# Bias matmuls over 128 rows, the softmax exchange spaced out, and an earlier turn of two x tiles, in a two-layer hybrid decoder

## The chip, the cores and the metric

The kernel runs on one core of a Trainium2 chip. The core has a matmul engine (TensorE, PE in the profile; its weight loads are listed as PEld), VectorE (DVE), ScalarE (ACT), GpSimd (POOL) and a sync engine (SP) that here only issues transfers. Each engine works through its own instructions in order; they meet at semaphores. Transfers are issued on the queues of SP, POOL and ACT. The metric is the time of one launch on the device, in microseconds (us), lower being better.

## The reference

Two layers over one sequence of 512 tokens of width 1024, in fp32. What matters here:

```
z = x @ w_in + b_in                    # 1024 -> 11648 columns, then split
q_a, k_a, v_a, q_r, k_r, v_r, g_r, gate_a, gate_b = split(z)
# (A) three groups of 6 heads of 64: causal windows (128, dilation 1), (512, 4), (2048, 16)
o_g, lse_g = attention(q_a, k_a, v_a)  # per group: output and log of the softmax denominator
y_a = sum_g softmax(lse)_g * o_g       # groups weighed by their denominators
# (B) retention, 4 heads: rotated q, k of 256, v of 512, chunks of 128, group norm
y_b = silu(g_r) * retention(q_r, k_r, v_r)
merged = sigmoid(gate_a) * (y_a @ w_attn_proj) + sigmoid(gate_b) * (y_b @ w_ret_proj)
x = layer_norm(alpha * x + merged @ w_out)
x = layer_norm(alpha * x + (silu(x @ w_gate) * (x @ w_up)) @ w_down)   # 2816 wide
```

The biases b_in are eight times as large as drawn, so they count in the result.

## The kernel before

**Numbers in two parts.** An fp32 value is held as a high part, rounded to the fast matmul format (fp32r), and a low part, the rest. `hilo` (L91) makes them: ScalarE casts the high part (L92), VectorE subtracts it from the source (L93). A product then takes three matmuls (`mm3`, L83): high by high, high by low, low by high. All of them go through the one line L81. x is held transposed as `xh` and `xl`, weights in `whi` and `wlo` (4 buffers each), loaded to `raw` (8 buffers of 512 KB). The source only gives an order of preference: a planner at compile time places each instruction on its engine's list by what its cost model thinks is ready.

**Seven products for eight.** The columns for v (attention) and for v and the swish gates (retention) are made by `tall` (L358): a Strassen form with seven products of half size. `ORDER` (L290) lists them: the left factors are parts of x or sums of such (`xs`), the right ones are the loaded blocks B11, B21, B22 and the sums P1 (B11 and B12), P2, P3 (B12 and B22) and P4. `Right` (L295) loads them on SP's queue; P1 and P3 are summed by a second, accumulating load on POOL's queue (L310), P2 and P4 by VectorE (L336) in P1's buffer. In `begin` (L332) all loads are asked for at once, B22 ahead of P3; B22 is the right factor of the fourth product and P3 that of the sixth. Three accumulators run along (`CHAIN`, L292), each opened by its first product.

**The bias.** It is added by one more matmul at the head of two of the chains (L369 to L371): `ones` as the stationary operand and `bh` as the moving one. Only two of their 33 rows hold anything: row 0 has the high part of the bias, row 32 the low part, and `ones` is 1 in these two rows and 0 elsewhere. `bias_rows` (L399) makes `bh`: POOL clears 33 rows (L403), four small transfers bring the two bias rows (L405, L406), VectorE adds (L407), ScalarE casts (L409), VectorE makes the low part in row 32 alone (L411). Each call of `biased` has 4 such matmuls; it is called twice a layer for attention's v (288 columns, the V stage) and four times for retention (512 columns): 48 in all.

**Side work.** Attention's own steps are threaded between weight matmuls: they stand in a list `side`, and `tick` (L133) takes from it at a rate that `pace` sets as steps per us. Attention runs in 3 pairs of heads (hp). For each pair `attention_pair` makes steps `scores` (L476: matmuls, VectorE's minimum L492, ScalarE's Exp L494), `turn` (L497: transposes, ScalarE copies to `sT` L503) and `values` (L506: matmuls, copies to `y` L513), and then weighs the two orders of tokens in which its groups run against each other. Tokens of the two orders sit on different partitions, so the statistics go through DRAM and back (the exchange), on ScalarE's queue:

- `swap` (L522) writes maxima and sums (L527); `swapped` reads them in the other order (L530) to `mb`.
- `weigh` (L532): VectorE's L536 to L538, ScalarE's Exp L539, VectorE's L540 to L544, a write of the weights `wb` (L545), and VectorE's `fa` for the first order (L546).
- `weighed` (L548) reads the weights in the other order (L549).
- `scale(0)`, `scale(1)` (L553) multiply `y` by them; `place(0)`, `place(1)` (L555) transpose `y` (L558) and put or add it into `yaT` (L560, L563).

The steps from `swapped` on are the tail; a pair's tail is worked in among the steps of the next pair at fixed places (L776), and the last pair's tail during the first retention head (L782).

**The start of layer 0** (L677 to L710). SP loads two x tiles, the four 128-column parts of the first q/k weights, the third x tile, the weights of the second group, and the fourth x tile. `to_xT` (L159) turns an x tile in two halves: four transposes, the cast of `xh`, the subtraction for `xl`, and a copy `xc` (L174) that is needed later for the sums. The first weights' parts are cast in `pair_units` (L196) when their loads are asked for; then tile 0 is turned, and tile 1 is the first entry of the side list, taken when the first matmul needs it (`need`, L151).

Of the kernel before, what the change touches and what calls it, by code (L numbers as in the profile page):

```python
# [18 lines left out]
P = 128  # L19
# [26 lines left out]
NEG = -1e30  # L46
L0, L1 = 383, 255
WARM = 3
BK = 33
FPARTS = ((0, 6), (6, 14), (14, 22))  # L50


# [1 line left out]
def hybrid_kernel(ctx, tc, x, rel_bias, w_in, b_in, w_attn_proj, w_ret_proj, w_out,  # L54
# [12 lines left out]

    ident = keep.tile([P, P], F32, name="ident")
    mhalf = keep.tile([P, 1], F32, name="mhalf")
    ones = keep.tile([BK, P], F32R, name="ones")  # L70
    bh = keep.tile([BK, 1024], F32R, name="bh")
    xh = keep.tile([P, KD, S], F32R, name="xh")
    xl = keep.tile([P, KD, S], F32R, name="xl")
    xs = keep.tile([P, 4, 2, 4, 256], F32R, name="xs")
# [16 lines left out]
    def hilo(src, hi, lo):  # L91
        act.copy(out=hi, in_=src)  # L92
# [11 lines left out]
    def view(t, a, b):  # L104
        return t[:, :a * b].rearrange("p (a b) -> p a b", a=a)
# [6 lines left out]
    def unit(v):  # L112
        a, b = v.shape[1], v.shape[2]
        h = view(wp.tile([P, 1024], F32R, tag="whi", name="whi"), a, b)
        l = view(wp.tile([P, 1024], F32R, tag="wlo", name="wlo"), a, b)
        hilo(v, h, l)
        return h, l
# [75 lines left out]
        return [[view(raw("xc"), 4, 256) for _ in range(2)] for _ in range(2)]  # L193


    def pair_units(w, c, c2=None, apart=False):  # L196
# [9 lines left out]
        if c2 is not None:  # L206
            todo = [(hf, q) for hf in range(2) for q in range(2)]
            for hf, q in sorted(todo, key=lambda t: t[::-1]) if apart else todo:
                nc.sync.dma_start(vs[hf][:, :, q * P:(q + 1) * P], w[:, 4 * hf:4 * hf + 4, (c, c2)[q]:(c, c2)[q] + P])
        if not apart:  # L210
            return [unit(v) for v in vs]
        out_ = [tuple(view(wp.tile([P, 1024], F32R, tag=t, name=t), 4, 256) for t in ("whi", "wlo")) for _ in vs]
        for q in range(2):
            for v, (h, l) in zip(vs, out_):
                cs = slice(q * P, (q + 1) * P)
                hilo(v[:, :, cs], h[:, :, cs], l[:, :, cs])
        return out_

    def part_of(us, k, q):
        h, l = us[k // 4]  # L220
# [74 lines left out]
    class Right:  # L295
# [33 lines left out]
        def begin(self, n):  # L329

            if n == "B11":
                self.load("B11", "B21", "P1", "B22", "P3")  # L332
            elif n in ("P2", "P4"):
                for u in range(len(self.shapes)):
                    r = self.t["P1", u]
                    dve.tensor_tensor(out=r, in0=r, in1=self.t["B22" if n == "P2" else "B21", u], op=ALU.add)  # L336
            return self.high(n)
# [61 lines left out]
    def bias_rows(b1, b2):  # L399

        n = b1.shape[0]
        r = raw("rb")[:BK, :2 * n]
        pool.memset(r, 0.0)  # L403
        for q in (0, BK - 1):
            pool.dma_start(r[q:q + 1, :n], b1.unsqueeze(0))  # L405
            pool.dma_start(r[q:q + 1, n:], b2.unsqueeze(0))  # L406
        dve.tensor_tensor(out=r[:, n:], in0=r[:, n:], in1=r[:, :n], op=ALU.add)  # L407
        h = bh[:, :2 * n]
        act.copy(out=h, in_=r)  # L409
        e = slice(BK - 1, BK)  # L410
        dve.tensor_tensor(out=h[e], in0=r[e], in1=h[e].bitcast(F32), op=ALU.subtract)  # L411
        return h

# [55 lines left out]
    def attention_pair(hp, qk, v, yp, bias, yaT):  # L469
# [104 lines left out]
            if t == 0:  # L574
                ops += [nothing] * 2
        ops.append(swap)
        tail = [swapped, weigh, weighed, lambda: scale(0), lambda: place(0), lambda: scale(1), lambda: place(1)]
        return ops, tail

    VB = 288  # L580
# [12 lines left out]
    def layer(ly, cp):  # L593
# [65 lines left out]
        with stage("attn") as ap_, stage("attw", 4) as aw:  # L659
# [2 lines left out]
            def qk_slot(hp, g):  # L662
                qk[hp, g] = opp.tile([P, 2, S], F32, tag="op", name="qk")

            def qk_units(hp, g, apart=False):
                c = g * GW + hp * P
                return pair_units(w_l, C_QA + c, C_KA + c, apart)

            def qk_put(hp, g, j, ps):
                cc = (C_QA, C_KA)[j] + g * GW + hp * P  # L670
# [6 lines left out]
            if ly == 0:  # L677
                x0 = [slot("x0", F32) for _ in range(NI)]
                warm = work("warm")
                dve.memset(warm, 0.0)  # L680
                px = psum()

                for _ in range(WARM):
                    mm(px, warm[:, :P], warm, True, True)
                act.dma_start(ident, c_id)

                def load_x(i):
                    for hf in range(2):
                        nc.sync.dma_start(x0[i][:, hf], x[i * P:(i + 1) * P, hf * S:(hf + 1) * S])

                load_x(0)
                load_x(1)
                for l_ in range(DEPTH):
                    pool.dma_start(braws[l_], b_in[l_].rearrange("(a b) -> a b", b=P))
                vecs = bias_vectors([aw.tile([P, S], F32, tag="bias", name="hot") for _ in range(NG)])
                us0 = [qk_units(0, 0, True)]
                load_x(2)
                us0.append(qk_units(0, 1))
                load_x(3)
                cp = x_copies()  # L700
                ops = [to_xT(x0[i].rearrange("p a b -> p (a b)"), i, cp) for i in range(NI)]
                for f in ops[0]:
                    f()
                side.extend(ops[1] + [lambda l_=l_: bias_cols(l_) for l_ in range(DEPTH)] + vecs[:3] + ops[2] + vecs[3:] + ops[3])
                o32 = work("o32")
                dve.memset(o32[:BK, :P], 0.0)
                dve.memset(o32[0:1, :P], 1.0)
                dve.memset(o32[BK - 1:BK, :P], 1.0)
                act.copy(out=ones, in_=o32[:BK, :P])
                rate[0], credit[0] = 0.4, 0.0  # L710
            else:
                us0 = [qk_units(0, g) for g in range(2)]
# [386 lines left out]
```

## Time and profile before

| what | value |
|---|---|
| time, median of 3 runs | 2248.61 us (2247.89 to 2251.42) |
| the profiled execution | 2250.18 us |
| its span, first to last instruction | 2248.4 us |
| TensorE busy | 2223.7 us (99%), 10890 matmuls |
| VectorE, ScalarE, POOL busy | 1184.3, 844.7, 180.8 us |
| mean granted TensorE clock | 0.997 |
| HBM traffic | 131 GB/s over the span |

Times in a timeline are us from the span's start: a row gives the start, the busy time, the engine, the line and operation, what is written from what, the tile's shape, and in brackets how long the engine was idle before it and what ended that. TensorE's matmuls overlap in their pipeline, so a row's busy time is longer than the distance to the next start; the distance is what the engine spends on it. A letter q after an engine marks its queue of transfers. In a table of stretches the columns are the stretch, its length, the busy time and count of PE, PEld, DVE, ACT and POOL, the granted clock as a share of full speed, the busy share of the DMA engines and the GB/s moved.

### The profile page before, as it was taken

What the parts mean: (1) busy time and instruction counts of PE and PEld (TensorE: products, weight loads), DVE (VectorE), ACT (ScalarE), POOL (GpSimd) and SP (SyncE); (2) the same over time, 40 slices, a digit from 0 to 9 for tenths busy, and PEclk for the clock granted to TensorE, in tenths of its full rate; (3) what the DMA queues carried; (4) which work ended last, traced back from release to release, by engine and by line L of the source; (5) the groups of instructions that cost most, each with busy time, mean ns of one, the idle gap of its engine ahead of it and who ended that gap; (6) DMA issues with size and microseconds to landing.
All of it is one profiled execution on the core that took longest, in us unless ns stands there. A gap on an engine that the chain in (4) does not pass through costs nothing.

```text
span 2248.4 us, 27714 instructions
## 1 busy us (share of the span) xinstructions
PE 2223.7 (99%) x10890; PEld 1841.0 (82%) x10890; DVE 1184.3 (53%) x1795; ACT 844.7 (38%) x1373; POOL 180.8 (8%) x240
## 2 busy tenths in 40 slices
PE   8999999999999999999999999999999999999998
PEld 7977778878888888888889777788888888888886
DVE  5643677776245543334376446777743455333345
ACT  4444544545333132223145445445543232222230
POOL 3110011110000100000030100111000001000001
PEclk9999999999999999999999999999999999999999
DMA  7943365555655133333159343565455552333320
GB/s 213 240 128 83 74 161 151 140 133 158 216 178 187 57 113 94 94 95 111 47 155 248 98 91 86 146 167 144 125 172 195 193 169 66 101 89 101 103 76 38
DMA packets 261602, 294.23 MB, mean 131 GB/s; under 512 B 21517, under 2 KB 199841, under 8 KB 261344
## 3 DMA queue, kind: packets, MB, share of 16 engines
q1 hardware_dynamic: 212928, 234.13, 35.0%
q0 software_dynamic: 21264, 45.54, 9.1%
q10 hardware_dynamic: 27280, 12.80, 2.0%
q8 instruction: 85, 1.39, 0.3%
q14 instruction: 45, 0.37, 0.1%
HBM read 266.63 MB, written 28.53 MB: 131 GB/s over the span
## 4 chain that ended last, share of the span: by engine, by line
PE 74%; issue 16%; DMA 4%; DVE 3%; POOL 1%; ACT 1%; POOLq 0%; DVEq 0%; ACTq 0%
PE ps L81 66%; PE px L81 6%; DMA raw<-in_w_in 2%; PE px L502 1%; POOL ry L124 1%; PE px L833 1%; DMA exd<-wb 1%; DMA fa<-exd 1%; DVE wlo L325 1%; DVE xtok L926 1%; DMA rb<-in_b_in 0%; DMA exd<-pk 0%; DMA mb<-exd 0%; DVE stats L937 0%; PE px L169 0%
## 5 line engine op out<-in xcount | busy, mean ns | idle before, releaser
L81 PE MATMUL ps<-xh,whi 128*128 128x512 f32 (+1 forms) x1760 | 674.8, 385 | 7.1 <-ACT xh L92 7.1
L81 PE MATMUL ps<-xh,wlo 128*128 128x512 f32 (+1 forms) x1760 | 659.7, 375 | 1.0 <-DVE wlo L93 1.0
L81 PE MATMUL ps<-xl,whi 128*128 128x512 f32 (+1 forms) x1760 | 659.6, 375 | 0.2 <-DVE xl L93 0.2
L93 DVE TENSOR_TENSOR wlo<-raw,whi 128x1024 fp32r<-128x1024 f32 (+2 forms) x274 | 330.8, 1208 | 528.2 <-ACT whi L92 527.7
L92 ACT CAST whi<-raw 128x1024 fp32r<-128x1024 f32 (+2 forms) x274 | 282.8, 1035 | 462.9 <-PE ps L81 399.6
L81 PEld LDWEIGHTS ps<-xh,whi 128*128 128x128 f32 x1760 | 332.1, 189 | 71.3 <-ACT xh L92 8.3
L81 PEld LDWEIGHTS ps<-xh,wlo 128*128 128x128 f32 x1760 | 332.2, 189 | 61.2 <-DVE wlo L93 1.2
L81 PEld LDWEIGHTS ps<-xl,whi 128*128 128x128 f32 x1760 | 333.1, 189 | 53.7 <-DVE xl L93 1.0
L81 PE MATMUL ps<-whi,xs 128*128 128x512 f32 (+1 forms) x768 | 221.9, 363 | 0.0
L325 DVE TENSOR_TENSOR wlo<-raw,whi 128x1024 fp32r<-128x1024 f32 (+1 forms) x168 | 178.7, 1064 | 81.1 <-ACT whi L319 80.3
L319 ACT CAST whi<-raw 128x1024 fp32r<-128x1024 f32 (+1 forms) x168 | 154.2, 923 | 118.8 <-PE ps L81 92.6
L81 PE MATMUL ps<-whi,ht 128*128 128x512 f32 x576 | 178.3, 389 | 0.0
L81 PEld LDWEIGHTS ps<-whi,xs 128*128 128x128 f32 x768 | 137.7, 188 | 24.1 <-ACT whi L319 2.2
L81 PE MATMUL ps<-wlo,xs 128*128 128x512 f32 (+1 forms) x384 | 138.0, 359 | 0.4 <-DVE wlo L325 0.4
L124 POOL TENSOR_TENSOR ry<-ve,mhalf 128x1 f32<-128x1 f32 x48 | 44.8, 944 | 1152.0 <-DVE ve L123 1152.0
L81 PEld LDWEIGHTS ps<-whi,ht 128*128 128x128 f32 x576 | 108.1, 188 | 22.4
L81 PE MATMUL ps<-wlo,ht 128*128 128x512 f32 x288 | 112.0, 389 | 0.0
L81 PE MATMUL ps<-whi,xh 128*128 128x512 f32 (+1 forms) x288 | 106.7, 370 | 1.9 <-DVE sn L429 1.9
L81 PE MATMUL ps<-wlo,xh 128*128 128x512 f32 (+1 forms) x288 | 103.2, 358 | 0.0
L81 PE MATMUL ps<-whi,xl 128*128 128x512 f32 (+1 forms) x288 | 103.0, 358 | 0.0
L310 POOL DMA_DIRECT2D raw<-in_w_in x48 | 59.2, 1234 | 293.0 <-DMA raw<-in_w_in 204.0
L81 PEld LDWEIGHTS ps<-wlo,xs 128*128 128x128 f32 x384 | 72.2, 188 | 9.6 <-DVE wlo L325 0.9
(167 smaller groups left out, 2518.9 us busy)
## 6 DMA issues: line engine op xcount, KB each, us to landing
raw<-in_w_in SPq DMA_DIRECT2D x144, 512.0 KB, 4.0
raw<-in_w_ffn_gate SPq DMA_DIRECT2D x44, 512.0 KB, 3.8
raw<-in_w_ffn_up SPq DMA_DIRECT2D x44, 512.0 KB, 3.8
raw<-in_w_ffn_down SPq DMA_DIRECT2D x44, 512.0 KB, 3.7
raw<-in_w_in SPq DMA_DIRECT2D x72, 256.0 KB, 5.3
raw<-in_w_in POOLq DMA_DIRECT2D x32, 512.0 KB, 7.4
raw<-in_w_ret_proj SPq DMA_DIRECT2D x32, 512.0 KB, 3.9
raw<-in_w_in SPq DMA_DIRECT2D x40, 288.0 KB, 4.3
```

The costliest lines, as they stand in the source:

```text
L81: pe.matmul(ps, lhsT=a, rhs=b, start=start, stop=stop, skip_group_check=True)
L92: act.copy(out=hi, in_=src)
L93: dve.tensor_tensor(out=lo, in0=src, in1=hi.bitcast(F32), op=ALU.subtract)
L124: pool.tensor_tensor(out=y, in0=ve, in1=mhalf, op=ALU.pow)
L310: pool.dma_start(r, self.src({"P1": "B12", "P3": "B22"}[n], u), accum_op=ALU.add)
L319: act.copy(out=h, in_=src)
L325: dve.tensor_tensor(out=l, in0=src, in1=h.bitcast(F32), op=ALU.subtract)
L502: pe.transpose(px[:, (2 + j) * P:(3 + j) * P], s[:, hh, j * P:(j + 1) * P], ident)
L833: pe.transpose(px[:, t * P:(t + 1) * P], ys[i][:, t * P:(t + 1) * P], ident)
L926: dve.scalar_tensor_tensor(out=o_, in0=o_, scalar=rs, in1=b_[:, c:c + n], op0=ALU.mult, op1=ALU.add)
```

## The change

Four things are edited.

- The tiles `ones` and `bh`, the cleared raw tile and its casts have 128 rows. Row 0 and row 32 hold the same as before, the other rows are zero.
- The tail's steps have another order and other places: `scale(0)` and `place(0)` now come before `weighed`. Among the next pair's steps `weigh` is put in at 12, not 8, `weighed` at 18, not 12, and the rest at 14, 16, 24 and 26; after the last pair there are more empty steps between.
- At the start of layer 0 tiles 0 and 1 of x are both turned before the first weights' parts are cast; the loads are asked for in the same order as before. The parts' function is now `pair_apart`, which gives the casts back as a function to be called later.
- In `begin`, P3 is loaded ahead of B22.

```diff
-BK = 33
+BK = 32
...
-    ones = keep.tile([BK, P], F32R, name="ones")
-    bh = keep.tile([BK, 1024], F32R, name="bh")
+    ones = keep.tile([P, P], F32R, name="ones")
+    bh = keep.tile([P, 1024], F32R, name="bh")
...
+    def pair_apart(w, c, c2):
+
+        vs = [view(raw(), 4, 256) for _ in range(2)]
         out_ = [tuple(view(wp.tile([P, 1024], F32R, tag=t, name=t), 4, 256) for t in ("whi", "wlo")) for _ in vs]
-        for q in range(2):
-            for v, (h, l) in zip(vs, out_):
-                cs = slice(q * P, (q + 1) * P)
-                hilo(v[:, :, cs], h[:, :, cs], l[:, :, cs])
-        return out_
+        parts = [(hf, slice(q * P, (q + 1) * P), cc) for q, cc in enumerate((c, c2)) for hf in range(2)]
+        for hf, cs, cc in parts:
+            nc.sync.dma_start(vs[hf][:, :, cs], w[:, 4 * hf:4 * hf + 4, cc:cc + P])
+
+        def make():
+            for hf, cs, _ in parts:
+                hilo(vs[hf][:, :, cs], out_[hf][0][:, :, cs], out_[hf][1][:, :, cs])
+
+        return out_, make
...
-                self.load("B11", "B21", "P1", "B22", "P3")
+                self.load("B11", "B21", "P1", "P3", "B22")
...
-        r = raw("rb")[:BK, :2 * n]
+        r = raw("rb")[:, :2 * n]
         pool.memset(r, 0.0)
-        for q in (0, BK - 1):
+        for q in (0, BK):
...
-        e = slice(BK - 1, BK)
+        e = slice(BK, BK + 1)
...
-        tail = [swapped, weigh, weighed, lambda: scale(0), lambda: place(0), lambda: scale(1), lambda: place(1)]
+        tail = [swapped, weigh, lambda: scale(0), lambda: place(0), weighed, lambda: scale(1), lambda: place(1)]
...
-                us0 = [qk_units(0, 0, True)]
+                first, make = qk_units(0, 0, pair_apart)
                 load_x(2)
-                us0.append(qk_units(0, 1))
-                load_x(3)
                 cp = x_copies()
                 ops = [to_xT(x0[i].rearrange("p a b -> p (a b)"), i, cp) for i in range(NI)]
-                for f in ops[0]:
+                for f in ops[0] + ops[1]:
                     f()
-                side.extend(ops[1] + [lambda l_=l_: bias_cols(l_) for l_ in range(DEPTH)] + vecs[:3] + ops[2] + vecs[3:] + ops[3])
+                make()
+                us0 = [first, qk_units(0, 1)]
+                load_x(3)
+                side.extend([lambda l_=l_: bias_cols(l_) for l_ in range(DEPTH)] + vecs[:3] + ops[2] + vecs[3:] + ops[3])
                 o32 = work("o32")
-                dve.memset(o32[:BK, :P], 0.0)
+                dve.memset(o32[:, :P], 0.0)
                 dve.memset(o32[0:1, :P], 1.0)
-                dve.memset(o32[BK - 1:BK, :P], 1.0)
-                act.copy(out=ones, in_=o32[:BK, :P])
+                dve.memset(o32[BK:BK + 1, :P], 1.0)
+                act.copy(out=ones, in_=o32[:, :P])
...
-                for at, f in zip((24, 22, 15, 14, 12, 8, 3), reversed(tail)):
+                for at, f in zip((26, 24, 18, 16, 14, 12, 3), reversed(tail)):
...
-            side.extend(n * 3 + tail[:1] + n * 4 + tail[1:2] + n * 3 + tail[2:5] + n * 6 + tail[5:6] + n * 2 + tail[6:])
+            side.extend(n * 3 + tail[:1] + n * 8 + tail[1:2] + n + tail[2:3] + n + tail[3:4] + n * 3 + tail[4:5] + n * 7 + tail[5:6] + n * 2 + tail[6:])
```

More of the change, by code (lines that the diff above doesn't have):

```diff
@@ L193, in x_copies, with pair_units @@
         return [[view(raw("xc"), 4, 256) for _ in range(2)] for _ in range(2)]
-    def pair_units(w, c, c2=None, apart=False):
+    def pair_units(w, c, c2=None):
         vs = []
@@ L205, in pair_units @@
                 vs.append(view(raw(), 4, 256))
[L206 to L211, printed above, removed]
-        out_ = [tuple(view(wp.tile([P, 1024], F32R, tag=t, name=t), 4, 256) for t in ("whi", "wlo")) for _ in vs]
-        for q in range(2):
-            for v, (h, l) in zip(vs, out_):
-                cs = slice(q * P, (q + 1) * P)
-                hilo(v[:, :, cs], h[:, :, cs], l[:, :, cs])
-        return out_
+                for q, cc in enumerate((c, c2)):
+                    nc.sync.dma_start(vs[hf][:, :, q * P:(q + 1) * P], w[:, ks, cc:cc + P])
+        return [unit(v) for v in vs]
+    def pair_apart(w, c, c2):
+        vs = [view(raw(), 4, 256) for _ in range(2)]
+        out_ = [tuple(view(wp.tile([P, 1024], F32R, tag=t, name=t), 4, 256) for t in ("whi", "wlo")) for _ in vs]
+        parts = [(hf, slice(q * P, (q + 1) * P), cc) for q, cc in enumerate((c, c2)) for hf in range(2)]
[5 more added lines that the diff above has]
+        return out_, make
     def part_of(us, k, q):
@@ L663, in qk_slot, with qk_units @@
                 qk[hp, g] = opp.tile([P, 2, S], F32, tag="op", name="qk")
-            def qk_units(hp, g, apart=False):
+            def qk_units(hp, g, how=pair_units):
                 c = g * GW + hp * P
-                return pair_units(w_l, C_QA + c, C_KA + c, apart)
+                return how(w_l, C_QA + c, C_KA + c)
             def qk_put(hp, g, j, ps):
```

## The prediction

> **What bounds the kernel now.** I read the cores, then the engines on the page, then the groups of the tile "bh", and then the timeline of each engine at the places that the diff touches.
>
> ```profile
> core 0: 2248.4 us, clock 0.997
> PE 2223.7 (99%) x10890; PEld 1841.0 (82%) x10890; DVE 1184.3 (53%) x1795; ACT 844.7 (38%) x1373; POOL 180.8 (8%) x240
> ```
>
> TensorE bounds it. Its 99% is made of modelled, overlapping ends, so lost time doesn't show there; it shows in the distance from one matmul's start to the next. An edit is worth what it takes out of these distances, and work on another engine counts only where TensorE waits for it. The profiled execution took 2250.18 us round its span of 2248.4; it is 1.57 over the median of the runs, 2248.61.
>
> **The bias matmuls: -18.9 us.** First a chain that opens without a bias (the second row), then the same with one:
>
> ```profile
> 334.79 0.39 PE L81 MATMUL ps<-whi,xl 128*128 128x512 f32 x1
> 335.02 0.39 PE L81 MATMUL ps<-whi,xh 128*128 128x512 f32 x1
> 335.25 0.39 PE L81 MATMUL ps<-wlo,xh 128*128 128x512 f32 x1
> ...
> 340.23 0.39 PE L81 MATMUL ps<-whi,xl 128*128 128x512 f32 x1
> 340.55 0.50 PE L81 MATMUL ps<-bh,ones 33*128 33x512 f32 x1
> 340.98 0.50 PE L81 MATMUL ps<-whi,xs 128*128 128x512 f32 x1
> 341.31 0.39 PE L81 MATMUL ps<-wlo,xs 128*128 128x512 f32 x1
> ```
>
> Two steps from 334.79 to 335.25 take 0.46, 0.23 each, and opening a new chain (335.02) costs nothing. Three steps from 340.23 to 341.31 take 1.08. So one bias matmul of 512 columns costs 0.40 us (1.08 less three of 0.227, the unrounded step) beyond its own place. With 288 columns, in the V stage:
>
> ```profile
> 87.53 0.29 PE L81 MATMUL ps<-wlo,xh 128*128 128x288 f32 x1
> 87.67 0.29 PE L81 MATMUL ps<-whi,xl 128*128 128x288 f32 x1
> 87.89 0.39 PE L81 MATMUL ps<-bh,ones 33*128 33x288 f32 x1
> ...
> 88.45 0.30 PE L81 MATMUL ps<-wlo,xs 128*128 128x288 f32 x1
> ```
>
> From 87.67 to 88.45 are 0.78 against three steps of 0.133 (as from 87.53 to 87.67): 0.38 lost. How many there are, and the work that prepares their rows:
>
> ```profile
> L81 PE MATMUL ps<-bh,ones x48: 393/498/502, 56.0 to 1603.1; 33*128 33x512 f32 x32, 33*128 33x288 f32 x16
> L409 ACT CAST bh<-rb x12: 669/1043/1050, 49.5 to 1546.4; 33x1024 fp32r<-33x1024 f32 x8, 33x576 fp32r<-33x576 f32 x4
> ```
>
> 32 x 0.40 + 16 x 0.38 = 18.9 us, all of it in TensorE's own order, with no other engine named ahead of these rows. What sets these 48 apart from the chain at 335.02 is the 33 rows, so I take the whole sum; the trace has no bias matmul over 128 rows, and the ends are 0 (it isn't the rows) and 19.3 (48 x 0.402). Against the trace's cause I hold two sentences of the Trainium skill. TensorE: Matmul & The Clock Gate, "Why this matters for your kernels", says that a matmul over 32 rows takes the time of one over 128, by which this term would be 0. TensorEngine Tiling, "Tiling Modes", says that a change of tiling mode drains the engine, by which it stands at 18.9, and the rows at 340.55 and 340.98, late on both sides, side with it. The casts, the clearing and the sums of the rows get 95 partitions more; the shortest cast above, 33x576, takes 669 ns, and one of 128x512 takes 620 (the row at 8.68, below), so rows cost nothing there and columns do.
>
> **The start: -2.5 us.** TensorE turns both tiles early and then waits:
>
> ```profile
> 6.12 2.32 PE L169 MATMUL px<-ident,x 128*128 128x128 f32 x16
> 14.51 0.58 PE L81 MATMUL ps<-xh,whi 128*128 128x256 f32 x1 [6.07 <-ACT xh L92]
> ...
> 6.76 0.59 ACT L92 CAST xh<-px 128x512 fp32r<-128x512 f32 x1 [4.00 <-PE px L169]
> 8.68 0.62 ACT L92 CAST whi<-raw 128x512 fp32r<-128x512 f32 x1 [1.34 <-DMA raw<-in_w_in]
> 10.39 0.62 ACT L92 CAST whi<-raw 128x512 fp32r<-128x512 f32 x1 [1.09 <-DMA raw<-in_w_in]
> 10.92 0.58 ACT L92 CAST xh<-px 128x512 fp32r<-128x512 f32 x1
> ...
> 13.35 0.62 ACT L92 CAST whi<-raw 128x512 fp32r<-128x512 f32 x1 [0.43 <-DMA raw<-in_w_in]
> 13.88 1.06 ACT L92 CAST xh<-px 128x512 fp32r<-128x512 f32 x2
> 14.83 1.57 ACT L174 COPY xc<-px 128x512 f32<-128x512 f32 x3
> ```
>
> The transposes are done at 8.44, yet ScalarE stands in order behind four weight parts that land late, and the last two x casts run at 13.88. The change gives the x casts the earlier place. With their copies beside them, ScalarE needs from 6.76 four casts of 0.59 and four copies of 0.52 (1.57/3): 11.2; the first part, landed by 8.68, is then cast by 11.8, and TensorE starts about 12.0 instead of 14.51: 2.5. The last of the four, landed by 13.35, is cast by 13.97 as before, and its matmuls come last. The ends are 0 (the planner keeps its order) and 4.7 (copies last, first part cast by 9.8). I take 2.5, as copies stand next to their casts in the source. Every load keeps its place in SP's queue, and the two x operations leave the side list for a place before any matmul, so nothing else moves up.
>
> **The exchange: -0.3 us.** The dearest wait of attention is in layer 0, pair 2:
>
> ```profile
> 203.73 0.17 DVE L536 TENSOR_TENSOR mn<-nm,mb 128x8 f32<-128x8 f32 x1 [4.04 <-DMA mb<-exd]
> ...
> 200.18 0.21 ACT L513 COPY y<-px 128x64 f32<-128x64 f32 x1 [3.18 <-PE px L81]
> 204.21 0.21 ACT L539 ACTIVATE ea<-ea 128x16 f32<-128x16 f32 x1 [3.81 <-DVE ea L538]
> 204.33 0.19 ACT L513 COPY y<-px 128x64 f32<-128x64 f32 x1
> ...
> 202.77 0.40 PE L81 MATMUL ps<-xh,wlo 128*128 128x512 f32 x1
> 206.21 1.43 PE L81 MATMUL px<-v,sT 128*128 128x64 f32 x8 [3.04 <-ACT sT L503]
> ...
> 207.00:210.00 3.00, 3.00 (x9) 2.52 (x10) 1.23 (x1) 0.71 (x3) 0.00 (x0) 0.50 0.15 8
> ```
>
> VectorE waits for the maxima's read, ScalarE's Exp for VectorE, the casts of sT behind Exp, TensorE for sT: 3.2 us (206.21 - 202.77 less a step). Then the granted clock is 0.50 for 3 us, which loses 1.5 more: 4.7. The Trainium skill, TensorE: Matmul & The Clock Gate, "Why this matters for your kernels", says that an idle stretch of over some 3 us halves the clock; the window agrees with its 0.50. The change puts weigh four steps later in the source. But Exp stands between two copies that the source writes back to back inside one values step, so the planner doesn't keep the source's order: it has lifted weigh to where it thinks the read has landed. The swap and its read are not moved, so it will lift weigh to the same place, and I count 0 there; the places' transposes, one and two steps later, find their operands lifted with it; the ends are -4.7, and +4.7 for each exchange that is quiet now and would wait like this one. After pair 2 the list (41 steps of the pair and the tail) grows from 66 steps to 73 over the same 42 us, so a step comes each 0.575 instead of 0.636: weigh goes from 31.8 (the 50th) to 31.1 (the 54th), the first place from 35.6 (56th) to 33.4 (58th), the last stays at 42.
>
> ```profile
> 263.88 0.68 DVE L553 TENSOR_TENSOR y<-y,fa 128x512 f32<-128x512 f32 x1
> ...
> 267.27 0.49 PE L558 MATMUL px<-ident,y 128*128 128x128 f32 x3
> ...
> 273.63 0.39 PE L81 MATMUL ps<-whi,xs 128*128 128x512 f32 x1
> 274.14 0.63 PE L558 MATMUL px<-ident,y 128*128 128x128 f32 x4
> ```
>
> The first place comes 2.2 earlier and its operand perhaps only 0.7, which takes 1.5 of the 2.7 us that lie between 264.56 and 267.27; no new wait. The last place now waits 0.28 (0.51 less a step) for a read that sets out earlier once the swap does: that goes. weighed is a DMA in ScalarE's queue and holds the casts behind it until the weights are written; it now stands behind the first place's copy instead of before it, which can only free that copy. No exchange DMA is on SP's or POOL's queue.
>
> **P3 loaded ahead of B22: 0.** Four pairs' transfers swap places in SP's queue, and POOL's two accumulating loads for P3 set out sooner. B22 now lands where P3 did, in the V stage from the last issue at 80.36 plus a median of 5.4:
>
> ```profile
> 80.36 0.38 SPq L109 DMA_DIRECT2D raw<-in_w_in  x1
> raw<-in_w_in SPq DMA_DIRECT2D x8, 288.0 KB, 5.4
> 88.98 0.68 PE L81 MATMUL ps<-whi,xs 128*128 128x288 f32 x2
> 90.06 0.40 PE L81 MATMUL ps<-wlo,xs 128*128 128x288 f32 x1 [0.40 <-DVE wlo L325]
> 80.00:90.00 10.00, 9.67 (x62) 8.31 (x61) 3.79 (x6) 4.25 (x9) 3.56 (x3) 1.00 1.01 230
> ```
>
> That is 85.8; B22's product comes after P1's, which starts at 87.89. What is late there already is P1 (the wait before 90.06, 0.7). The ends: -0.7, and +0.7 if P3's loads hold P1 back as long again.
>
> **Sum.** 2250.18 - 18.9 - 2.5 - 0.3 = 2228.5; less the 1.57 by which this execution is over the median: 2226.9, rounded 2227.
>
> **Rivals.** (A) The exchange's wait goes, by the new spacing or because the read misses the heavy transfers: 4.7 more, 2222. For it: it needs one slow landing. Against: the planner's lifting. (B) Loads bind the V stage. For it: DMA share 1.01 at 80 to 90 and the wait for P1; TensorE, earlier by 2.5 and by 16 x 0.38/2 = 3.0 in layer 0, would only wait longer. It gives back up to 5.5: 2232. Against: loads are issued when slots come free, which follows TensorE. (C) The loss isn't of the rows but of a bias operand as such (by the first sentence of the skill above, too): 2250.18 - 2.8 - 1.57 = 2246. Against: late on both sides, and chains without a bias open free. (D) Slower: the two reads of each of the six exchanges (mb and fa) meet ScalarE's queue so that each holds it until its landing, as mb does at 203 now, TensorE idle and then at half clock, 4.7 each. From the fifth new one on, 23.5 outweighs the 21.7 saved; with all eleven 2279. Against: fa is read by VectorE alone, and the waits follow one slow landing.
>
> **How the numbers follow.** Forecast 47%, A 28%, B 19%, C 4%, D 2%. The range runs from 2219 (A with a start of 4.7) to 2234 (B, with an exchange move worth a little less than nothing); it leaves out C, D and the tails. A run of this kernel can't be told from no change within 0.2%, 4.5 us: forecast, A and B are all faster by more, 0.94; C is the same, 0.04; D slower, 0.02.
>
> **What would show it.** Bias rows of the form 128*128 with the next two matmuls 0.23 us apart; if they stay late on both sides, C. The first xh,whi matmul near 12; if it stands at 14.5, the planner kept its order. Exp still standing between copies in pair 2 of layer 0, with or without a wait before sT. The wait for wlo in the V stage's second product of P1: above 0.7 it is B. Wrong would be a time above 2234 with all bias rows quick, for then TensorE's saving was taken back by a wait that I haven't seen.

## The result, and the profile after

The changed kernel takes 2236.03 us (median of 4 runs, 2232.78 to 2237.54); the kernel before took 2250.02 beside it (2247.89 to 2251.77). The ratio is 0.9936, with a 95% interval of 0.9919 to 0.9954: 14.0 us less, where 21.7 were forecast. At 2236 it lies above the range, which ended at 2234.

Lines of the code behind the diff stand four or more further down than in the prediction: the accumulating load is L314, the low parts of `tall` L329, the first step of weigh L540, scale L557, place L562, the scores on VectorE L496 and their Exp L498.

The cores and the engines on the page of the kernel after:

```profile
core 0: 2235.8 us, clock 0.996
PE 2209.1 (99%) x10890; PEld 1843.1 (82%) x10890; DVE 1182.8 (53%) x1795; ACT 842.1 (38%) x1373; POOL 181.4 (8%) x240
```

The group of its bias matmuls (durations in ns, least, median and greatest), and two stretches of TensorE's timeline (start, duration, engine, line, operation, tiles, rows x columns):

```profile
L81 PE MATMUL ps<-bh,ones x48: 292/389/479, 53.2 to 1590.8; 128*128 128x512 f32 x32, 128*128 128x288 f32 x16
```

```profile
77.83 0.30 PE L81 MATMUL ps<-bh,ones 128*128 128x288 f32 x1
77.96 0.29 PE L81 MATMUL ps<-whi,xh 128*128 128x288 f32 x1
78.10 0.29 PE L81 MATMUL ps<-wlo,xh 128*128 128x288 f32 x1
...
325.96 0.39 PE L81 MATMUL ps<-xh,wlo 128*128 128x512 f32 x1
326.19 0.39 PE L81 MATMUL ps<-bh,ones 128*128 128x512 f32 x1
326.42 0.39 PE L81 MATMUL ps<-whi,xh 128*128 128x512 f32 x1
```

The bias matmul now takes its own place and nothing more: 0.23 to either side with 512 columns, 0.13 with 288. The start has moved too, as the timelines of TensorE and ScalarE show:

```profile
6.77 2.34 PE L169 MATMUL px<-ident,x 128*128 128x128 f32 x16
12.41 0.38 PE L81 MATMUL ps<-xh,whi 128*128 128x256 f32 x1 [3.30 <-ACT whi L92]
```

```profile
10.22 1.62 ACT L174 COPY xc<-px 128x512 f32<-128x512 f32 x3
11.65 2.38 ACT L92 CAST whi<-raw 128x512 fp32r<-128x512 f32 x4
```

ScalarE casts and copies all of x's first two tiles, and then casts the four weight parts back to back: the first product starts at 12.41, not 14.51. So both terms are there, and yet a third of the sum is missing. Where it went, the waits of TensorE in the V stage of layer 0 tell first (what was waited for and who released it, total us, times, longest), then the timelines of TensorE and ScalarE there:

```profile
PE ps L81 <- ACT whi L323: 1.0, 2, 0.8
PE ps L81 <- DVE wlo L329: 0.8, 2, 0.4
```

```profile
83.23 0.40 PE L81 MATMUL ps<-whi,xs 128*128 128x288 f32 x1 [0.18 <-ACT whi L323]
84.03 0.40 PE L81 MATMUL ps<-wlo,xs 128*128 128x288 f32 x1 [0.40 <-DVE wlo L329]
85.75 0.40 PE L81 MATMUL ps<-whi,xs 128*128 128x288 f32 x1 [0.80 <-ACT whi L323]
86.54 0.61 PE L81 MATMUL ps<-wlo,xs 128*128 128x288 f32 x1 [0.39 <-DVE wlo L329]
```

```profile
82.51 0.67 ACT L323 CAST whi<-raw 128x576 fp32r<-128x576 f32 x1 [4.08 <-DMA raw<-in_w_in]
85.03 1.82 ACT L323 CAST whi<-raw 128x576 fp32r<-128x576 f32 x3 [1.55 <-DMA raw<-in_w_in]
```

Two windows around them (length, then busy time and count of PE, PEld, DVE, ACT and POOL, the granted clock, the DMA share, GB/s), and the two accumulating loads of P1 among the DMA issues (median us to landing at the end):

```profile
80.00:86.00 6.00, 4.62 (x30) 3.88 (x29) 1.79 (x3) 1.95 (x4) 0.00 (x0) 1.00 1.17 229
86.00:89.40 3.40, 3.01 (x13) 2.86 (x13) 3.22 (x6) 1.24 (x3) 0.00 (x0) 0.52 0.42 115
```

```profile
raw<-in_w_in POOLq DMA_DIRECT2D x2, 288.0 KB, 8.6
```

Before, this place had one wait of 0.40. Now there are four: two behind the cast at 82.51 and two behind the one at 85.03, which waited for the halves of P1 to land. P1 is finished by a second, accumulating load on POOL's queue, and its two halves take 8.6 us to land here. Then the clock is 0.52 for 3.4 us.

The second place is the attention pair at 200 us, where before a read of the maxima had cost 3.2 us and half the clock. The timelines of VectorE, of ScalarE with its queue and of TensorE, then the windows:

```profile
199.90 0.17 DVE L540 TENSOR_TENSOR mn<-nm,mb 128x8 f32<-128x8 f32 x1 [3.73 <-DMA mb<-exd]
...
208.21 1.23 DVE L93 TENSOR_TENSOR wlo<-raw,whi 128x1024 fp32r<-128x1024 f32 x1 [2.66 <-ACT whi L92]
209.60 0.69 DVE L557 TENSOR_TENSOR y<-y,fa 128x512 f32<-128x512 f32 x1 [0.16 <-DMA fa<-exd]
210.21 0.28 DVE L496 CUSTOM_DVE_ANT_0 s<-px,bias 128x128 f32<-128x128 f32 x1
```

```profile
202.16 0.38 ACTq L549 DMA_DIRECT2D exd<-wb  x1
...
206.75 0.34 ACTq L553 DMA_DIRECT2D fa<-exd  x1
207.13 1.05 ACT L92 CAST whi<-raw 128x1024 fp32r<-128x1024 f32 x1 [3.28 <-PE ps L81]
```

```profile
209.17 0.39 PE L81 MATMUL ps<-xh,wlo 128*128 128x512 f32 x1
211.08 0.71 PE L506 MATMUL px<-ident,s 128*128 128x128 f32 x2 [1.52 <-ACT s L498]
```

```profile
209.00:212.00 3.00, 1.42 (x7) 0.77 (x6) 1.54 (x6) 1.31 (x6) 1.19 (x1) 1.00 0.43 115
212.00:215.40 3.40, 3.40 (x17) 2.52 (x15) 1.72 (x6) 1.19 (x5) 1.18 (x1) 0.56 0.97 175
215.40:219.00 3.60, 3.60 (x13) 2.88 (x12) 0.38 (x1) 1.17 (x4) 0.00 (x0) 0.50 1.03 178
```

The wait for mb is still there on VectorE (3.73), but no longer TensorE's. Its place was taken by the other read, of the weights to fa. ScalarE issues it at 206.75, when the write of the weights (issued at 202.16) has landed 4.6 us later, and its next cast stands behind that issue, at 207.13; the profile names for this cast a matmul that frees its buffer. VectorE has three things ahead of the scores on its list: it waits 2.66 for this cast, makes the low part, waits 0.16 for fa, and makes the second scale. The wait for fa and the scale are 0.8 us of that. TensorE had made the scores at 206.80; VectorE comes to them at 210.21, their Exp and their turn come after that, and TensorE loses 1.7 us (211.08 - 209.17 less a step) and then, at a clock of 0.56 and 0.50, 0.44 x 3.4 + 0.50 x 3.6 = 3.3 more. Layer 1 has the same chain at the same place of its attention stage. There the cast is put down to the write of the weights itself, and the wait for fa is longer:

```profile
1314.23 1.05 ACT L92 CAST whi<-raw 128x1024 fp32r<-128x1024 f32 x1 [2.15 <-DMA exd<-wb]
...
1315.31 1.23 DVE L93 TENSOR_TENSOR wlo<-raw,whi 128x1024 fp32r<-128x1024 f32 x1 [1.54 <-ACT whi L92]
1317.57 0.69 DVE L557 TENSOR_TENSOR y<-y,fa 128x512 f32<-128x512 f32 x1 [1.04 <-DMA fa<-exd]
```

The scores come next on VectorE; TensorE waits 1.3 us for their Exp, and, some ten us earlier, 1.0 us for sT behind the read of mb.

### The profile page after: what moved, and what is told of

It is laid out like the page before. It is cut to its first block, busy times and chain, and to the rows that moved or that the text cites. A ratio compares the mean times of both kernels' runs of the same rounds, so it can differ in the third digit from the quotient of the medians.

```text
span 2235.8 us, 27732 instructions
## 1 busy us (share of the span) xinstructions
PE 2209.1 (99%) x10890; PEld 1843.1 (82%) x10890; DVE 1182.8 (53%) x1795; ACT 842.1 (38%) x1373; POOL 181.4 (8%) x240
## 4 chain that ended last, share of the span: by engine, by line
PE 72%; issue 19%; DMA 4%; DVE 3%; POOL 1%; ACT 1%; SPq 0%; POOLq 0%; DVEq 0%; ACTq 0%
PE ps L81 64%; PE px L81 6%; DMA raw<-in_w_in 2%; PE px L506 1%; PE px L838 1%; POOL ry L124 1%; DMA exd<-wb 1%; DVE xtok L931 0%; DMA mb<-exd 0%; DMA exd<-pk 0%; DMA rb<-in_b_in 0%; DVE wlo L329 0%; PE px L169 0%; DVE stats L942 0%; DVE xl L93 0%
## 5 line engine op out<-in xcount | busy, mean ns | idle before, releaser
L329 DVE TENSOR_TENSOR wlo<-raw,whi 128x1024 fp32r<-128x1024 f32 (+1 forms) x168 | 178.8, 1065 | 67.4 <-ACT whi L323 66.5
L81 PE MATMUL ps<-xs,whi 128*128 128x512 f32 x256 | 78.8, 389 | 0.0
```

The costliest lines, as they stand in the source:

```text
L81: pe.matmul(ps, lhsT=a, rhs=b, start=start, stop=stop, skip_group_check=True)
L329: dve.tensor_tensor(out=l, in0=src, in1=h.bitcast(F32), op=ALU.subtract)
```

## The experiments

Three groups: parts of the change alone or undone; one suspected wait taken away at a time; and the change's terms measured again with both waits gone. The kernel before ran beside each group, at medians of 2249.81, 2250.27 and 2251.81, so a difference in us between kernels of two groups is sure to some 2 us.

**The rows alone.** The kernel before with the 128 rows and nothing else:

```diff
-BK = 33
+BK = 32
-    ones = keep.tile([BK, P], ...); bh = keep.tile([BK, 1024], ...)
+    ones = keep.tile([P, P], ...);  bh = keep.tile([P, 1024], ...)
```

> The kernel before with the bias tiles over 128 rows and nothing else changed. Theory (the drain of 33 rows is worth 48 x 0.40 = 19 us, and only the later edits give some of it back): 17 to 19.5 us faster than the kernel before, bias matmuls with 0.23 us on both sides, V stage waits of at most 1.5 us in each layer. Rival (the V stage is bound by its loads, so TensorE's saving there only becomes waiting): 13 to 15.5 us faster, with some 2 to 3 us of new waits before wlo or whi in the V stage of each layer.

2237.43 (2236.09 to 2243.14), ratio 0.9949 (0.9936 to 0.9961): 12.4 us, not 18.9, and even less than the rival's 13 to 15.5. The two retention stages take 5.0 and 5.1 less, the V stage of layer 1 takes 1.2 less. The V stage of layer 0 takes as long as before, though its seven steps between the first and the last bias matmul became 7 x 0.38 = 2.7 shorter; these rows of TensorE's waits there show why:

```profile
PE ps L81 <- ACT whi L319: 1.4, 2, 0.9
PE ps L81 <- DVE wlo L325: 0.8, 2, 0.4
```

So it is the saving itself, not the other edits, that meets the loads. The loads did not follow TensorE: the stage begins 0.4 us later and TensorE saves 0.38 at each of six bias matmuls ahead of P1's last product, yet the accumulating loads of P1 for it set out when they did before (POOL's timeline, before and then with the rows alone; the second half sets out at 80.52 and 80.51):

```profile
77.98 1.26 POOL L310 DMA_DIRECT2D raw<-in_w_in  x1 [10.53 <-DMA raw<-in_w_in]
...
78.14 1.26 POOL L310 DMA_DIRECT2D raw<-in_w_in  x1 [10.61 <-DVE sn L429]
```

**The change without its parts.** B22 loaded ahead of P3 again; the exchange's steps as close as before; 33 rows again:

```diff
-                self.load("B11", "B21", "P1", "P3", "B22")
+                self.load("B11", "B21", "P1", "B22", "P3")
```

> The changed kernel with B22 loaded ahead of P3 again. Theory (P3's early accumulating loads share the engines with P1's, which land later): 3 to 5 us faster than the changed kernel, the 3.0 us of waits in the V stage of layer 0 and the 1.9 us in layer 1 gone but for 0.7. Rival (the V stage is bound by its bytes in any order): within 1 us of the changed kernel, and the same waits at other matmuls.

```diff
-        tail = [swapped, weigh, scale(0), place(0), weighed, scale(1), place(1)]
+        tail = [swapped, weigh, weighed, scale(0), place(0), scale(1), place(1)]
-                zip((26, 24, 18, 16, 14, 12, 3), reversed(tail))
+                zip((24, 22, 15, 14, 12, 8, 3), reversed(tail))
```

> The changed kernel with the tail's old order and places. Theory (the planner lifts the exchange's reads whatever the source says, so the spacing only trades the wait for mb against one for fa): within 2 us of the changed kernel, a wait of 2 to 5 us in pair 2 of layer 0 in both. Rival (the new spacing itself made the wait for fa at scale): 3 to 6 us faster than the changed kernel. Second rival (the new spacing had removed the wait for mb): 3 to 6 us slower.

```diff
-BK = 32; ones [P, P], bh [P, 1024]
+BK = 33; ones [BK, P], bh [BK, 1024]
```

> The changed kernel with the bias tiles over 33 rows again. Theory (the rows are worth 19 us on TensorE, of which the changed kernel's V stage gives some 4 back): 14 to 16 us slower than the changed kernel, V stage waits back to below 1 us. Rival (the rows are worth less than their gaps because the weight loads hide them): under 10 us slower.

They give 2233.76 (2229.48 to 2237.28; 0.9927, 0.9914 to 0.9939), 2236.04 (2234.63 to 2240.73; 0.9941, 0.9928 to 0.9955) and 2247.77 (2245.83 to 2252.00; 0.9992, 0.9984 to 1.0001), beside 0.9936 of the whole change. The rows are 12.6 us of it (0.0056 of 2250), between the expectation's theory and its rival. The spacing of the exchange is worth nothing in all, though it moves the wait: with the old one TensorE waits 2.8 us for sT in layer 0, with the new one 1.5 for s. The old order of loads may be 2 us better, but the intervals overlap, and its theory fails in layer 0: the V stage takes 34.7 us with either order, and 1.3 us of waits remain in it. What does differ is how long the accumulating loads take. For the last columns of layer 0's V stage, the two of P1 took 7.6 us with the old order and the two of P3 5.5 (first and second row); in the kernel after P1's took 8.6 (above) and P3's 9.9 (third row):

```profile
raw<-in_w_in POOLq DMA_DIRECT2D x2, 288.0 KB, 7.6
raw<-in_w_in POOLq DMA_DIRECT2D x2, 288.0 KB, 5.5
...
raw<-in_w_in POOLq DMA_DIRECT2D x2, 288.0 KB, 9.9
```

**Are the loads the V stage's bound?** In the kernel after, the accumulating loads are left out there; in the next run VectorE makes the sums instead, from four blocks loaded once:

```diff
-                    if n in ("P1", "P3"):
+                    if n in ("P1", "P3") and self.acc:     # acc False in the V stage
                         pool.dma_start(r, self.src(...), accum_op=ALU.add)
```

> The kernel after, with the two accumulating loads that finish P1 and P3 left out in the V stage alone (P1 is then B11's neighbour as first loaded; the products read incomplete weights, so part of V is not computed). Theory 1: these loads, which land 8 to 10 us after their issue, bind the V stage, and took back what its quick bias matmuls gave: from the first to the last bias matmul of the V stage 34.7 us become about 31.8 in layer 0 and 33.4 about 31.5 in layer 1; the whole some 4 to 5 us below the kernel after. Rival: the stage is bound by what makes the weights (VectorE, ScalarE) or by the rows of the bias: unchanged within 1 us, the waits keep their place before the product with P1.

```diff
-                self.load("B11", "B21", "P1", "P3", "B22")
+                self.load("B11", "B21", "B12", "B22")       # in the V stage
+            elif n[0] == "P":                               # P1, P2, P4 in B11's buffer, P3 in B12's
+                dve.tensor_tensor(out=r, in0=r, in1=<other block>, op=ALU.add)
```

> The kernel after; in the V stage alone the four blocks are loaded once (8 transfers of 288 KB a column pair instead of 14, none accumulating), and VectorE makes P1 and P3 by adding in place before it splits them. The whole reference is computed. Theory 1 (late accumulating loads bind the V stage): the waits before P1's product go, the stage becomes 31.5 to 33 us in both layers, the whole 3 to 5 us below the kernel after, and below it by as much as the run without the loads, if VectorE's four added sums a column pair stay hidden. Rival: VectorE's sums stand in front of the splits and take the place of the wait: no change within 1 us, and VectorE named as the releaser.

2226.11 (2224.80 to 2227.56; 0.9891, 0.9875 to 0.9908) and 2227.58 (2227.17 to 2227.98; 0.9898, 0.9883 to 0.9913): 10 and 8.5 us under the kernel after. The V stages fall to 31.3 and 31.3 in the one, 31.5 and 31.3 in the other, from 34.7 and 33.4, and TensorE waits for nothing in them. The ten microseconds that held the four waits in the kernel after are, without the loads:

```profile
80.00:90.00 10.00, 10.00 (x77) 10.00 (x76) 8.03 (x13) 5.17 (x9) 0.00 (x0) 1.00 0.61 177
```

The theory holds: it is the loads, and VectorE's sums stay hidden; the gain is twice what was expected. (The form with VectorE's sums also has fewer transfers, 8 for 14; the one without the accumulating loads keeps the ten plain ones.) Between the profiled spans lie 11.2 us without the loads, and the V stages give 5.5 of them. The rest comes in the stages behind them: 3.0 in the first attention stage, whose stand of 1.6 us is still there but isn't followed by the low clock, and 2.6 in the first retention stage; why these follow was not tried.

**Is the exchange what slows the attention stages?** A small VectorE operation whose operand is the running pair's last score keeps each read and each step that uses it from being lifted ahead of its place; in the next run the exchange's four transfers are left out, and with them the two small ScalarE copies that pack what is sent:

```diff
+            held[0] = nm[:, od, i, 1:2]                      # in scores
         def swapped():
+            dve.tensor_scalar(mb[:, 0, 0:1], held[0], 0.0, None, op0=ALU.mult)
             act.dma_start(mb, exd...)
+            # likewise: z ahead of weigh's first minimum and of scale(1), fa ahead of its read
```

> The kernel after, with the steps of the exchange that read the other core half's maxima and sums (mb, fa) tied by a false operand to the running pair's scores, so that the planner can't lift them ahead of where the source puts them; weigh one place earlier in the list. The arithmetic is the same, with seven small VectorE operations more a pair. Theory: in the kernel after VectorE stands at an operation that the planner lifted to before its read has landed, and the scores behind it, and so TensorE, wait: held back, the two attention stages lose these waits, 141.2 and 138.5 us become 134 to 137, the whole 3 to 8 us below the kernel after. Rival: the waits come from where the scores or the casts stand on their own: no change or up to 2 us slower from the added operations.

```diff
-            act.dma_start(exd..., pk); act.dma_start(mb, exd...)
-            act.dma_start(exd2..., wb); act.dma_start(fa[:, 1], exd2...)
+            dve.tensor_copy(fa[:, 1], wb)                    # weights from nm[:, 1], ls[:, 1]
```

> The kernel after with the four transfers of each exchange left out (each row's weights come from its own order of operations alone, so the merge of the two halves isn't computed). It prices all waits of the exchange together. Theory: they cost what the attention stages have above some 134 us: 141.2 and 138.5 fall to 133 to 135, the whole 8 to 11 us below the kernel after. Rival: the attention stages are slow for other reasons (the biases' columns, the scores): under 3 us.

2227.53 (2227.11 to 2230.82; 0.9901, 0.9886 to 0.9916) and 2225.12 (2224.47 to 2226.72; 0.9888, 0.9874 to 0.9903): 8.5 and 10.9 under the kernel after. Both have the attention stages at 135.5 in either layer, from 141.2 and 138.5. So holding the steps back wins all that taking the transfers away wins there, for 24 more operations on VectorE: four an exchange, not the seven of the expectation. With the steps held, TensorE has no wait in layer 0's attention stage, and the clock stays full there.

**The terms again, with both waits gone.** VectorE's sums in the V stage and the held exchange together (the expectations call the two waits covers, as they hide the gain); then the same with 33 rows; then with 33 rows and the old start; then, on the first, the old spacing:

```diff
 both:      the two edits above (sums on VectorE, exchange held)
 33 rows:   both, BK = 33
 old start: both, BK = 33, x's second tile on the side list, first parts cast ahead of it
 old tail:  both, with (24, 22, 15, 14, 12, 8, 3) and weighed behind weigh
```

> The kernel after with both covers taken away: the V stage's sums made by VectorE, not by accumulating loads, and the exchange's steps held where the source puts them. The whole reference is computed. Theory: the two waits are separate, so their prices add: 2236.0 - 8.5 - 8.5 = 2219, V stages 31.5, attention stages 135.5. Rival: they share a cause (one shifts the other, as the stages after the V stage came out faster without the loads), so the sum is less than the parts: 2223 to 2227.

> The run with both covers taken away, but with the bias matmuls over 33 rows as before. Theory: the prediction's term was right in size and only hidden, so with no wait to hand it to, 33 rows cost 18.9 us more than the run with both: 2238 if that is 2219, of it 3.0 in each V stage, 6.4 in each retention stage's four heads. Rival: TensorE's lost places overlap with something else, as between the kernel after and its 33-row form, 11.7: 2231.

> As the run with both covers taken away and 33 rows, and with the kernel before's start (x's second tile turned later, the first weights' parts cast ahead of it). Against the run that has only the 33 rows it prices the start alone. Theory: 2.5 us as predicted, all of it kept, since the V stage no longer waits for loads: first xh,whi matmul 14.5 instead of about 12. Rival: the next wait in the first product (second weight part, third and fourth tile of x) takes it back: under 1 us, with the stretch up to the first bias matmul longer by less than the start.

> The run with both covers taken away, but with the steps of the exchange as close together as before (weigh five steps behind its read, not eight, weighed straight behind it). Theory: once the planner can't lift them, distance matters, and the closer steps meet reads that haven't landed: 2 to 8 us slower than the run with both, in the attention stages, VectorE waiting for mb or fa. Rival: held by the running pair's scores the reads land in time at either distance: within 1 us.

They give 2220.60 (2220.16 to 2221.26), 2238.31 (2238.24 to 2238.68), 2240.95 (2239.51 to 2241.53) and 2220.48 (2220.01 to 2221.12), beside 2251.81 of the kernel before; the first's ratio is 0.9863 (0.9849 to 0.9876). The two waits' prices nearly add: 15.4 where 8.5 and 8.5 were found apart. The rows are worth 17.7, the start 2.6, and the spacing nothing, though its theory had 2 to 8 us. The run with both has no wait and no low clock in either place:

```profile
72.00:90.00 18.00, 18.00 (x138) 18.00 (x137) 14.62 (x23) 10.01 (x18) 0.00 (x0) 1.00 0.64 190
196.00:219.00 23.00, 23.00 (x134) 17.79 (x133) 12.11 (x36) 11.20 (x37) 2.37 (x2) 1.00 0.56 116
```

It beats both kernels: it is the change with the two waits taken away, 15 us below the change as it stands. Here one bias matmul of 33 rows against one of 128 is seen with nothing else around it (33 rows, then both):

```profile
77.67 0.29 PE L81 MATMUL ps<-whi,xl 128*128 128x288 f32 x1
77.89 0.39 PE L81 MATMUL ps<-bh,ones 33*128 33x288 f32 x1
78.21 0.40 PE L81 MATMUL ps<-whi,xh 128*128 128x288 f32 x1
78.45 0.30 PE L81 MATMUL ps<-wlo,xh 128*128 128x288 f32 x1
```

```profile
77.59 0.30 PE L81 MATMUL ps<-whi,xl 128*128 128x288 f32 x1
77.72 0.30 PE L81 MATMUL ps<-bh,ones 128*128 128x288 f32 x1
77.86 0.30 PE L81 MATMUL ps<-whi,xh 128*128 128x288 f32 x1
77.99 0.29 PE L81 MATMUL ps<-wlo,xh 128*128 128x288 f32 x1
```

Three steps are 0.78 in the one and 0.40 in the other. Set side by side from the profiled executions (us; the first stage begins with the span, the others at starts of TensorE's own rows: first and eighth bias matmul, first score, ninth and 24th bias matmul, and so in layer 1; the stages left out have waits under 0.1 us; "waits" is the difference of the two columns before it; "free" is the form with both waits taken away, for the kernel before that with 33 rows and old start, which has the new spacing and order of loads):

```
stage                       before   free    waits     after   free    waits
up to the first bias matmul  55.99   55.54    0.45      53.19   52.97    0.22
V, layer 0                   34.93   34.02    0.91      34.72   31.41    3.31
to the first score           19.05   19.05    0.00      19.48   18.75    0.73
attention, layer 0          139.18  135.59    3.59     141.24  135.47    5.77
retention, layer 0          244.75  241.65    3.10     238.57  236.25    2.32
V, layer 1                   34.13   34.02    0.11      33.40   31.30    2.10
attention, layer 1          135.66  135.60    0.06     138.52  135.49    3.03
retention, layer 1          244.37  243.05    1.32     237.33  237.90   -0.57
whole span                 2248.40 2238.74    9.66    2235.76 2218.76   17.00
```

Between the free forms lie 20.0 us, the worth of the rows and the start; the waits rise by 7.3; 12.6 are left between the two spans. Attention and retention rows of a layer go together: with the old spacing the free form has 1.4 us less in each attention stage and 1.5 more in each retention stage.

## Why the prediction was wrong, point by point

**The bound: right.** TensorE's steps decide throughout, and every change of time was found as steps between its starts.

**The bias matmuls: right in cause and nearly in size, wrong as a gain.** The cause is the 33 rows, since 128 rows have no loss on either side. With no wait around, they are worth 17.7 against the 18.9 of the sum, 0.37 each against 0.38 and 0.40. The V stages give all of their share there; the retention stages 5.4 and 5.1 between the first and the last of their 16 matmuls and 0.4 and 0.3 behind the last, less than 16 x 0.40 = 6.4. The sentence of the Trainium skill in TensorE: Matmul & The Clock Gate, "Why this matters for your kernels", by which 32 rows take the time of 128, would have made this term 0; the measurement decides against it for a lone 33-row matmul amid others, which costs 0.38 us of 288 columns. The Trainium skill's sentence in TensorEngine Tiling (Array Packing), "Tiling Modes", by which a change of mode drains the engine, fits, but no run separates a drain from any other cost of changing the row count.

The step that failed is the one that put the whole 18.9 into the sum as "in TensorE's own order, with no other engine named ahead of these rows". For the 16 of the V stage another resource was named three parts further down, the DMA share of 1.01 and the wait for P1. What TensorE saved there went to the loads of P1. **Rival B** was this mechanism, with up to 5.5 us; the waits of the V stages and of the stretch behind rose by 5.1 (2.4, 0.7, 2.0). That the two numbers are near is luck: B's 5.5 was the start's 2.5 and layer 0's 3.0, and the runs show layer 0's 3.1 and 2.0 of layer 1, which B left out, with the start's gain kept. B had 19% and should have been the main line: the argument against it, that loads are issued when slots come free and so follow TensorE, did not hold, for with the rows alone P1's loads set out at 78.14 and 80.51 instead of 77.98 and 80.52.

**The start: right.** 12.41 for 12.0, and 2.6 us for 2.5 where nothing waits behind it. In the kernel after it is kept too: the first score starts at 107.4 instead of 110.0, 2.6 us earlier, so up to there only the V stage's own share is lost.

**The exchange: right on weigh, wrong on the waits.** The new spacing is worth nothing (2220.48 with the old one against 2220.60 with the new; 0.9941 against 0.9936 without the held steps), and weigh was lifted as before, as the row at 199.90 shows. But the step "I count 0 there" took the wait of 4.7 to stay where it was, and no other exchange to wait anew. The edit moved it. In the three kernels with the old spacing and steps that aren't held (before, rows alone, old spacing again) the longest wait of TensorE in layer 0's attention is for sT, behind mb: 3.0, 2.3 and 2.8 us. In the five with the new spacing and steps that aren't held it is for s, behind the read of fa: 1.2 to 1.6. In layer 0 this cost as much as before, 1.7 + 3.3 = 5.0 for 4.7. In layer 1 all five have both waits, 1.0 and 1.3 in the kernel after; the three with the old spacing have one there, of 0.6, 1.0 and 3.2, so what the edit added in layer 1 is not settled. In the table the attention stages' waits rise by 5.1 and those of the retention stages fall by 2.7: some 2.5 us taken back in all. This is rival D in small, at three reads (fa in layer 0, mb and fa in layer 1) and not at eleven. D's counterargument called fa harmless because only VectorE reads it. But VectorE's list is where the scores stand, and ScalarE's casts stand behind the issue of the read.

**P3 ahead of B22: its 0 is not refuted.** With four accumulating loads out together it is mostly P3's own that take longer, 9.9 us instead of 5.5 where shown; P1's, which are needed first, take 8.6 instead of 7.6. Yet the V stage of layer 0 takes 34.7 us with either order, and that of layer 1 0.8 more with the new one. On the whole kernel that is between nothing and some 2 us.

**The sum.** 17.7 + 2.6 for 18.9 + 2.5 + 0.3, a miss of 1.4. Of the 9 us between 2227 and 2236 as much again is the kernel before, which ran at 2250.02 beside this one and not at 2248.61. The other 6 are waits that rose (7.3 between the profiled spans), 5.1 of them B's and some 2.5 the exchange's, which the prediction had counted as alternatives. They happened together, which neither the forecast nor a range cut at B held. "A time above 2234 with all bias rows quick" was named as what would show it wrong, and that is what came.

## What to carry to other kernels

A saving on the bounding engine counts only up to the next thing that this stage waits for: before it is summed, look in its own stage for the resource that is already full (a DMA share of 1, a wait of 0.4 us on a late load), and price the stage by that. A matmul of 33 rows amid ones of 128 cost 0.4 us here, on both sides of it, and the scores' matmuls over 64 rows show a like step ahead of them (206.48 to 206.80, where a step is 0.23); padding its operands with zeros to the common row count took that away at no price on TensorE. Where a scheduler places steps by its own guess of when a transfer lands, spacing in the source only moved the wait from one read to another; a real operand that arrives late enough holds a step in place, and here four small operations an exchange won 8.5 us.

## What the runs showed of the hardware that was not expected

**Accumulating loads out together take longer, the later ones above all.** The median from issue to landing of 288 KB was 6.0 to 6.1 us where B22's plain load stood between those of P1 and P3, and 7.6 to 8.5 where they went out together (512 KB: 7.3 to 7.5 against 8.2 to 8.6), over three kernels of the one order and five of the other. Taken apart, those of P1 had medians of 7.1 to 7.8 and of 7.5 to 8.1, P3's of 4.9 to 5.1 and 8.0 to 8.9. So what rises is mostly the time of the pair that was sent out behind the other. The plain load of 288 KB stays at 4.3 to 4.5.

**The clock after a short stand is not one rule.** In the kernel after, a stand with a wait of 1.52 us was followed by 6.8 us at half clock (212.4 to 219.3). In the run without the accumulating loads a stand of 1.6 us at the same place was not followed by any:

```profile
PE px L506 <- ACT s L498: 1.6, 1, 1.6
...
206.00:208.00 2.00, 1.16 (x5) 0.69 (x5) 0.41 (x4) 1.41 (x6) 0.86 (x2) 1.00 0.70 188
208.00:210.00 2.00, 2.00 (x17) 1.63 (x16) 1.13 (x5) 0.66 (x3) 1.18 (x1) 1.00 0.93 157
```

The Trainium skill, TensorE: Matmul & The Clock Gate, "Why this matters for your kernels", warns of idle stretches of over some 3 us; here half of that sufficed once and did nothing another time. Waits of 2.3 us (rows alone) and 2.8 us (old spacing) in the same stage were followed by no low clock either. So a stand must be priced with and without the loss behind it, 1.5 us (before) to 3.3 us (after) here. What decides between them, no run here shows.
